# Row sums of squares by products with a column of ones, and another order of loads, in the first stage of a hybrid diffusion backbone

## The chip, the cores and the metric

One core of one Trainium2 chip runs the whole kernel. The metric is the device time of one execution, in microseconds (us). TensorE is called PE here (its weight loads, which overlap its products, PEld), VectorE DVE, ScalarE ACT, GpSimd POOL, and SyncE, which issues most of the transfers, SP.

## What is computed

Two layers over 512 latent tokens x and 256 context tokens ctx, each 1024 wide. Every layer normalizes each token by the root of its mean square, scales and shifts it by vectors that come from a conditioning vector, and feeds a mixer; layer 0 is a retention mixer, layer 1 a gated MLP.

```python
def rmsnorm(x, g):
    y = x * lax.rsqrt(jnp.mean(x * x, axis=-1, keepdims=True) + NORM_EPS)
    return y * g

shift_x, scale_x, gate_x = jnp.split(silu(c) @ ada_w[i] + ada_b[i], 3, axis=-1)
shift_c, scale_c, gate_c = jnp.split(silu(c_ctx) @ ada_w[i] + ada_b[i], 3, axis=-1)
hx = rmsnorm(x, norm_g[i]) * (1 + scale_x) + shift_x
hc = rmsnorm(ctx, norm_g[i]) * (1 + scale_c) + shift_c
...
qx, kx, vx, zx = retention_project(hx, w_in)     # layer 0
qc, kc, vc, zc = retention_project(hc, w_in)
```

The change lies in what leads up to the first products of `retention_project` (the queries and keys of head 0).

## The kernel before, in words

All activations lie transposed: features on the 128 partitions, tokens along the free axis. x is kept as four tiles `xq[t, g]` (t: half of the tokens, 256 each; g: half of the features, four blocks of 128), ctx as two tiles `cq[g]`. Weights and activations are split into a high part (rounded to float32r, a cast on ACT) and a low part (the rest, a subtraction on DVE), and every product of weights is three products: low by high, high by low, high by high (`mm3`).

The first stage does, in the order of its text on each engine (PE, ACT and DVE are pinned to that order there):

- **Row sums.** `flips` transposes a 128-token piece of x with four PE transposes (against `ident`) into a PSUM bank, and `squares` takes the sum of squares along the free axis on ACT, with an accumulator. `inverse` adds the two halves, takes root and reciprocal; `spread` broadcasts the result over the partitions with a product against `ident` and copies it out (`rs[t]`). ctx gets the same in the loop, at kb = 2 and 3 (`half_rows`).
- **Conditioning.** `ada0_mm(kb)` multiplies the silu of both conditioning vectors (`cpad`) by a block of 1 MB of `ada_w`, eight products that use 32 columns of the array each; `ada0_cols(kb)` transposes the copied result with two transposes and makes, on DVE, the scale `gs0` and shift `sh0` for feature block kb.
- **Coming of a block.** `come((kb, th))` multiplies block kb of x by scale and `rs`, adds the shift into the high part on ACT, and makes the low part on DVE.
- **Plain products.** `plain(kb, th, nhs)` multiplies that block by its weights, six passes for each of two weight halves `nh` and each half `th` of tokens. The loop runs over kb = 1 to 7; products of ctx (`th` = 2) follow at kb = 5, 6, 7.
- **Fills.** `fill(n)` multiplies ones by ones n times: it computes nothing that is used. `N_WARM` = 10 stand at the start, 5, 4 and 5 more between the steps.

The weights of the stage are four blocks of 512 KB (B11, B12, B21, B22 of head 0), loaded by `Q.pump_n` and split whole by `Q.upto`. The order of transfers on SP's queue is the order of the calls: first tile of x, `ident`, second tile, `sv`, conditioning block 0, weight block, the other two tiles of x, weight block, conditioning blocks 1 to 3, ctx, and, from inside the loop, the rest. `ada0_load(kb)` puts block kb into a place that later holds something else (`ADA_AT`), so a later load waits for an earlier block's use.

Of the kernel before, what the change touches and what calls it, by code (L numbers as in the profile page):

```python
# [14 lines left out]
P = 128  # L15
D = 1024
# [52 lines left out]
def hybrid_kernel(ctx, tc, xT_d, cT_d, cv_d, sv_d, rows_d, ada0_d, adag_d, w_d, rope_d, dec_d, ws_d, id_d, out_d):  # L69
# [69 lines left out]
    class Stream:  # L139
# [3 lines left out]
        def __init__(self):  # L143
            self.items, self.loads, self.raws, self.left, self.tiles = [], [], {}, {}, {}
            self.free, self.stage, self.done, self.sent, self.at = [], 0, 0, 0, -1
            self.gate = self.limit = self.cap = None

# [10 lines left out]
        def load(self, key, slots, stage, parts):  # L158
            self.loads.append((key, slots, stage, parts))

# [274 lines left out]
    ADA_AT = ("oS1", "oS2", "oS4", "oA22", "oS1", "oS2", "oS4", ("w4", "g1"))  # L435
# [12 lines left out]
    load(xq[0, 0], xT_d[:, 0:4, 0:HS])  # L448
    load(ident, id_d)
    load(xq[0, 1], xT_d[:, 4:8, 0:HS])  # L450
    load(sv, sv_d)
    ada0_load(0)
    Q.stage = 1
    Q.pump_n(1)
    load_x(1)
    Q.pump_n(1)
    for kb in (1, 2, 3):
        ada0_load(kb)
    for g in range(2):
        load(cq[g], cT_d[:, 4 * g:4 * g + 4, :])  # L460
# [49 lines left out]
    def squares(pq, s):  # L510
        act.activation(t2("junk0"), pq, AF.Square, accum_out=s)

    def flips(src, g, i, s):

        pq = pt()
        for k in range(4):
            pe.transpose(pq[:, k * P:k * P + P], src(4 * g + k, i), ident)
        squares(pq, s[:, g, i:i + 1])
        return pq

    def inverse(s):
        dve.tensor_tensor(s[:, 0, :], s[:, 0, :], s[:, 1, :], ALU.add)
        act.activation(s[:, 1, :], s[:, 0, :], AF.Sqrt, bias=eps, scale=1.0 / D)
        dve.reciprocal(s[:, 1, :], s[:, 1, :])

    def spread(s, name):

        pr = pt((P, HS), tag="tm")
        for i in range(2):
            mm(pr[:, i * P:i * P + P], s[:, 1, i:i + 1].to_broadcast([P, P]), ident, start=True, stop=True)  # L530
# [14 lines left out]
    def ada0_cols(kb, e):  # L545
# [6 lines left out]
        dve.tensor_tensor(gs0[:, kb, :], s[:, 0, :], adab0[:, 1, kb, :], ALU.add)  # L552
        dve.tensor_tensor(sh0[:, kb, :], s[:, 1, :], adab0[:, 0, kb, :], ALU.add)
        dve.scalar_tensor_tensor(gs0[:, kb, :], gs0[:, kb, :], 1.0, g0[:, kb, :], ALU.add, ALU.mult)
# [70 lines left out]
    def half_rows(src, g, s):  # L625
        for i in range(2):
            flips(src, g, i, s)

    def by_half(src, name, n=0):
        s = sq[name] = st([P, 2, 2], f"sq{name}", name="sq")  # L630
        for g in range(2):
            half_rows(src, g, s)
            if g == 0:
                fill(n)
# [62 lines left out]
    for low in lows:  # L697
        low()
# [927 lines left out]
```

## Time and profile before

| | |
|---|---|
| median of 3 runs | 875.37 us (874.91 to 875.52) |
| the profiled execution | 875.18 us, its span 873.4 us |
| PE busy | 862.0 us, 99% of the span |
| DVE, ACT busy | 708.6 us, 472.3 us |
| moved | 153.80 MB, mean 176 GB/s |

The profile groups instructions by engine and by the names of their tiles. Busy time of PE is modelled, since products overlap; the start of a weight load is the better mark of when PE got to an instruction. Almost every line reads L55, the helper through which instructions go. In the trace a float32 product is two passes and counts twice; a transpose and a float32r product count once. In slices of 1/40 of the span the transfers are dense only in the first two:

```
DMA  9941761972695596758175722446435045045602
GB/s 332 393 136 62 241 219 59 301 253 97 213 370 145 192 314 220 258 167 303 42 254 188 232 85 77 146 167 217 146 122 176 17 146 191 7 142 194 94 28 97
```

### The profile page before, as it was taken

What the parts mean: (1) busy time and instruction counts of PE and PEld (TensorE: products, weight loads), DVE (VectorE), ACT (ScalarE), POOL (GpSimd) and SP (SyncE); (2) the same over time, 40 slices, a digit from 0 to 9 for tenths busy, and PEclk for the clock granted to TensorE, in tenths of its full rate; (3) what the DMA queues carried; (4) which work ended last, traced back from release to release, by engine and by line L of the source; (5) the groups of instructions that cost most, each with busy time, mean ns of one, the idle gap of its engine ahead of it and who ended that gap; (6) DMA issues with size and microseconds to landing.
All of it is one profiled execution on the core that took longest, in us unless ns stands there. A gap on an engine that the chain in (4) does not pass through costs nothing.

```text
span 873.4 us, 14635 instructions
## 1 busy us (share of the span) xinstructions
PE 862.0 (99%) x5670; PEld 777.3 (89%) x5670; DVE 708.6 (81%) x998; ACT 472.3 (54%) x763; POOL 62.6 (7%) x100
## 2 busy tenths in 40 slices
PE   8999999999999999999999999999999999999996
PEld 6898899898889888999989898888999899899895
DVE  2689979988696987878688869978898578779976
ACT  5466444553524576536362559785865455255345
POOL 0000210110121020000000010102000000000200
PEclk9999999999999999999999999999999999999999
DMA  9941761972695596758175722446435045045602
GB/s 332 393 136 62 241 219 59 301 253 97 213 370 145 192 314 220 258 167 303 42 254 188 232 85 77 146 167 217 146 122 176 17 146 191 7 142 194 94 28 97
DMA packets 77094, 153.80 MB, mean 176 GB/s; under 512 B 8032, under 2 KB 35040, under 8 KB 77024
## 3 DMA queue, kind: packets, MB, share of 16 engines
q1 hardware_dynamic: 68736, 128.53, 44.6%
q0 software_dynamic: 8000, 24.13, 8.4%
q8 instruction: 44, 0.72, 0.3%
q14 instruction: 26, 0.21, 0.1%
q10 hardware_dynamic: 288, 0.20, 0.1%
HBM read 128.71 MB, written 24.12 MB: 175 GB/s over the span
## 4 chain that ended last, share of the span: by engine, by line
PE 93%; ACT 2%; DVE 2%; DMA 2%; issue 0%; SPq 0%; ACTq 0%
PE pst L55 93%; DMA xq<-in_xT_dram 2%; DVE hl L55 1%; ACT hl L55 1%; ACT f L55 1%; ACT oA L55 0%; ACT junk L55 0%; DVE o L55 0%; DVE xq L55 0%; ACT o L55 0%; DVE cq L55 0%; DVE raw L55 0%; ACT oS L55 0%; DVE gs L55 0%; ACT fss L55 0%
## 5 line engine op out<-in xcount | busy, mean ns | idle before, releaser
L55 DVE TENSOR_TENSOR hl<-raw,hl 128x1024 fp32r<-128x1024 f32 x195 | 237.3, 1223 | 71.8 <-ACT hl L55 71.1
L55 ACT CAST hl<-raw 128x1024 fp32r<-128x1024 f32 x195 | 203.6, 1049 | 156.9 <-DVE raw L55 63.1
L55 PE MATMUL pst<-oS,hl 128*128 128x256 f32 x1104 | 134.1, 280 | 0.5 <-ACT oS L55 0.4
L55 PE MATMUL pst<-hl,oS 128*128 128x512 f32 x576 | 134.2, 390 | 0.1
L55 PEld LDWEIGHTS pst<-oS,hl 128*128 128x128 f32 x1104 | 130.9, 188 | 1.3 <-ACT oS L55 0.9
L55 PEld LDWEIGHTS pst<-hl,oS 128*128 128x128 f32 x576 | 107.9, 188 | 23.2 <-DVE oS L55 0.5
L55 PE MATMUL pst<-oA,hl 128*128 128x256 f32 x936 | 117.8, 281 | 0.2
L55 PEld LDWEIGHTS pst<-oA,hl 128*128 128x128 f32 x936 | 112.7, 188 | 2.4 <-issue 0.4
L55 DVE TENSOR_TENSOR raw<-raw 128x1024 f32<-128x1024 f32 x92 | 111.5, 1222 | 0.9
L55 PE MATMUL pst<-hl,oA 128*128 128x512 f32 x408 | 95.8, 390 | 0.0
L55 PE MATMUL pst<-og,hl 128*128 128x256 f32 x768 | 92.8, 280 | 0.0
L55 PEld LDWEIGHTS pst<-og,hl 128*128 128x128 f32 x768 | 90.9, 188 | 0.8 <-issue 0.4
L55 PEld LDWEIGHTS pst<-hl,oA 128*128 128x128 f32 x408 | 76.2, 188 | 15.5
L55 ACT COPY snap<-pst 128x512 f32<-128x512 f32 x84 | 49.1, 585 | 43.0 <-PE pst L55 41.9
L55 PE MATMUL pst<-hl,ya 128*128 128x512 f32 (+1 forms) x300 | 68.5, 381 | 0.0
L55 PEld LDWEIGHTS pst<-hl,ya 128*128 128x128 f32 x300 | 54.6, 188 | 10.7
L55 PE MATMUL pst<-v,ph 128*128 128x512 f32 x192 | 59.4, 391 | 0.0
L55 DVE TENSOR_TENSOR snap<-pst,snap 128x512 f32<-128x512 f32 x63 | 42.8, 688 | 5.7 <-PE pst L55 5.5
L55 ACT CAST ph<-pf 128x512 fp32r<-128x512 f32 x24 | 14.9, 620 | 52.1 <-DVE pf L55 49.7
L55 PEld LDWEIGHTS pst<-v,ph 128*128 128x128 f32 x192 | 36.1, 188 | 7.0
L55 DVE SCALAR_TENSOR_TENSOR acc<-pst,gate,acc 128x256 f32<-128x256 f32 x64 | 29.1, 480 | 13.6 <-PE pst L55 13.4
L55 PE MATMUL pst<-v,pl 128*128 128x512 f32 x96 | 37.9, 395 | 0.0
(196 smaller groups left out, 1011.9 us busy)
## 6 DMA issues: line engine op xcount, KB each, us to landing
raw<-in_w_dram SPq DMA_DIRECT2D x224, 256.0 KB, 4.2
bg<-in_adag_dram SPq DMA_DIRECT2D x32, 512.0 KB, 5.3
ada_w<-in_ada_dram SPq DMA_DIRECT2D x16, 512.0 KB, 8.7
raw<-in_w_dram SPq DMA_DIRECT2D x16, 512.0 KB, 3.7
bg<-in_dec_dram SPq DMA_DIRECT2D x12, 512.0 KB, 5.5
v<-snap POOLq DMA_DIRECT2D x16, 256.0 KB, 4.8
z<-snap POOLq DMA_DIRECT2D x16, 256.0 KB, 5.6
v<-v SPq DMA_DIRECT2D x8, 512.0 KB, 4.7
```

The costliest lines, as they stand in the source:

```text
L55: made = op(*args, **kw)
```

## The change

The squares are taken of x as it lies, on ACT for two of a tile's four blocks and on DVE for the other two; a product with the squares as stationary side and one column of ones as moving side then sums over features into a column of PSUM, for 128 tokens at a time, accumulated over both tiles. No transposes of x or ctx are left. All four tiles of x are loaded first on SP; `ident` and `sv` go to ACT's queue. The first two weight blocks are loaded in slices of columns (one, one, and two of their four 128-column groups) between conditioning blocks, and are split in the same slices. Block 0 and 1 of x are multiplied by `rs` before the scale is known (`ready`), and `first_come` applies scale and shift together on ACT. `ada0_mm` moves in PE's order, the third and fourth weight block are split later, ctx is loaded later and its row sums are taken at kb = 4. There are 61 fills in place of 24.

```diff
+        def begin(self, ks, parts):
+            k0, k1 = ks[0] * P, ks[-1] * P + P
+            for i, (b, kh) in enumerate(parts):
...
+                load(self.raws[key].rearrange("p (s n) -> p s n", s=2)[:, :, k0:k1],
+                     w_d[b:b + 2, :, kh * 512 + k0:kh * 512 + k1].rearrange("s p n -> p s n"))
+
+        def halve(self, i, ks, late=None):
...
+            split((part(hl[:, 0, :]), part(hl[:, 1, :])), part(self.raws[q, at]), late)
...
-    ADA_AT = ("oS1", "oS2", "oS4", "oA22", "oS1", "oS2", "oS4", ("w4", "g1"))
+    ADA_AT = ("oS1", "oS2", "oS4", "oA22", ("w4", "g1"), "oS1", "oS2", "oS4")
...
-    load(xq[0, 0], xT_d[:, 0:4, 0:HS])
-    load(ident, id_d)
-    load(xq[0, 1], xT_d[:, 4:8, 0:HS])
-    load(sv, sv_d)
+    nc.scalar.dma_start(ident, id_d)
+    nc.scalar.dma_start(sv, sv_d)
+    load_x(0)
+    load_x(1)
     ada0_load(0)
-    Q.stage = 1
-    Q.pump_n(1)
-    load_x(1)
-    Q.pump_n(1)
-    for kb in (1, 2, 3):
-        ada0_load(kb)
-    for g in range(2):
-        load(cq[g], cT_d[:, 4 * g:4 * g + 4, :])
+    Q.stage, Q.cap = 1, 2
+    FIRST = ((2, 0), (0, 0))
+    Q.begin((0,), FIRST)
+    ada0_load(1)
+    Q.begin((1,), FIRST)
+    ada0_load(2)
+    Q.begin((2, 3), FIRST)
+    ada0_load(3)
+    ada0_load(4)
...
+    def squares(src, g, sums):
+        for j in range(2):
+            y, x = t2("squares"), src[:, 2 * j:2 * j + 2, :]
+            if j == 0:
+                act.activation(y.rearrange("p (k n) -> p k n", k=2), x, AF.Square)
+            else:
+                dve.tensor_tensor(y.rearrange("p (k n) -> p k n", k=2), x, x, ALU.mult)
+            for k in range(2):
+                for i in range(2):
+                    mm(sums[i][:, 0:1], y[:, k * HS + i * P:k * HS + i * P + P], ones[:, 0:1], start=(g + j + k == 0),
+                       stop=(g + j + k == 3), skip_group_check=True)
...
+    def first_come(kb, th, lows=()):
...
+        act.activation(h, y, AF.Identity, bias=sh0[:, kb, 0:1], scale=gs0[:, kb, 0:1])
+        for low in lows:
+            low()
+        dve.tensor_scalar(f, y, gs0[:, kb, 0:1], None, ALU.mult)
+        dve.scalar_tensor_tensor(l, f, sh0[:, kb, 0:1], f32(h), ALU.add, ALU.subtract)
...
+    fill(12)
+    for th in range(2):
+        sq[th] = [pt() for i in range(2)]
+        for g in range(2):
+            squares(xq[th, g], g, sq[th])
+            fill(8)
+    for th in range(2):
+        sq[th] = inverse(sq[th], f"sq{th}")
+    for th in range(2):
+        rs[th] = spread(sq[th], f"rs{th}")
+    ready(0, 0)
+    ready(0, 1)
     es = ada0_mm(0)
+    lows = []
     ada0_cols(0, es)
+    fill(7)
+    Q.halve(0, (0,))
+    first_come(0, 0)
+    Q.halve(1, (0,), lows)
+    first_come(0, 1, lows)
+    ready(1, 0)
+    ready(1, 1)
+    plain(0, 0)
     es = ada0_mm(1)
+    Q.pump_n(2)
+    ada0_load(5)
+    for g in range(2):
+        load(cq[g], cT_d[:, 4 * g:4 * g + 4, :])
+    for i in (0, 1):
+        Q.halve(i, (1,))
     plain(0, 1, (0,))
     ada0_cols(1, es)
+    first_come(1, 0)
+    first_come(1, 1)
     plain(0, 1, (1,))
...
+    END = {2: 4, 3: 5, 4: 6}
     for kb in range(1, 8):
         if kb == 3:
-            Q.upto(4)
-        plain(kb, 0)
-        if kb + 1 < 8:
+            Q.upto(3)
+        if kb < 3:
+            plain(kb, 0, (0,))
+            es = ada0_mm(kb + 1)
+            plain(kb, 0, (1,))
+        else:
+            plain(kb, 0)
+        if kb < 7:
             ada0_cols(kb + 1, es)
             come((kb + 1, 0), (kb + 1, 1))
-        if kb in (2, 6, 7):
-            Q.upto({2: 3, 6: 5, 7: 6}[kb])
+        if kb == 5:
+            es = ada0_mm(7)
+        if kb == 1:
+            for i in (0, 1):
+                Q.halve(i, (2, 3))
+        if kb in (3, 6, 7):
+            Q.upto({3: 4, 6: 5, 7: 6}[kb])
+        if kb == 4:
+            sq[2] = [pt((P, HS), tag="tm") for i in range(2)]
+            for g in range(2):
+                squares(cq[g], g, sq[2])
+            sq[2] = inverse(sq[2], "sq2")
         plain(kb, 1)
-        if kb + 2 < 8:
-            es = ada0_mm(kb + 2)
+        if kb in END:
+            es = ada0_mm(END[kb])
...
-        if kb in (2, 3):
-            half_rows(rows_c, kb - 2, sq[2])
```

Three places in the engines' orders follow, as they stand. First PE, from its first instruction to the first plain products (`oA` and `oS` are the high and low parts of x for the two halves of tokens, `hl` the split weights, `adae` the copied conditioning product). Before:

```order
L55 MATMUL pst<-ones 128x128 x10
L55 MATMUL pst<-ident,xq 128x128 x8
L55 MATMUL pst<-ones 128x128 x5
L55 MATMUL pst<-ident,xq 128x128 x8
L55 MATMUL pst<-ada_w,cpad 32x256 x8
L55 MATMUL pst<-ones 128x128 x4
L55 MATMUL pst<-ident,sq 128x128 x2
L55 MATMUL pst<-ident,adae 128x128 x2
L55 MATMUL pst<-ident,xq 128x128 x16
L55 MATMUL pst<-oA_250,hl 128x256 x6
```

The same place on PE in the changed kernel, first its start:

```order
L55 MATMUL pst<-ones 128x128 x22
L55 MATMUL pst<-ones,squares 128x1 x8
L55 MATMUL pst<-ones 128x128 x8
L55 MATMUL pst<-ones,squares 128x1 x8
L55 MATMUL pst<-ones 128x128 x8
```

and, after one more such pair of rows, from the last group of squares on:

```order
L55 MATMUL pst<-ones,squares 128x1 x8
L55 MATMUL pst<-ones 128x128 x8
L55 MATMUL pst<-ident,root 128x128 x4
L55 MATMUL pst<-ada_w,cpad 32x256 x8
L55 MATMUL pst<-ident,adae 128x128 x2
L55 MATMUL pst<-ones 128x128 x7
L55 MATMUL pst<-oA_336,hl 128x256 x12
```

Four groups of eight products with squares, each followed by eight fills, stand where transposes stood, and both spreads come ahead of the first conditioning product.

Second, DVE around the coming of block 2 (`ada_s` is the reduced conditioning, `gs` and `sh` scale and shift). Before:

```order
L55 TENSOR_REDUCE ada_s<-pst 128x4
L55 TENSOR_TENSOR gs_151<-ada_s,sv 128x2
L55 TENSOR_TENSOR sh_152<-ada_s,sv 128x2
L55 SCALAR_TENSOR_TENSOR gs_151<-gs_151,sv 128x2
L55 SCALAR_TENSOR_TENSOR xq<-xq,gs_151,rs_240 128x256
L55 SCALAR_TENSOR_TENSOR xq<-xq,gs_151,rs_306 128x256
L55 SCALAR_TENSOR_TENSOR oA_250<-xq,sh_152,oA_250 128x256
L55 SCALAR_TENSOR_TENSOR oS_308<-xq,sh_152,oS_308 128x256
L55 TENSOR_REDUCE ada_s<-pst 128x4
```

The same block on DVE in the changed kernel:

```order
L55 TENSOR_REDUCE ada_s<-pst 128x4
L55 TENSOR_TENSOR gs_155<-ada_s,sv 128x2
L55 SCALAR_TENSOR_TENSOR gs_155<-gs_155,sv 128x2
L55 TENSOR_TENSOR sh_156<-ada_s,sv 128x2
L55 SCALAR_TENSOR_TENSOR xq<-xq,gs_155,rs_296 128x256
L55 SCALAR_TENSOR_TENSOR xq<-xq,gs_155,rs_301 128x256
L55 SCALAR_TENSOR_TENSOR oA_336<-xq,sh_156,oA_336 128x256
L55 SCALAR_TENSOR_TENSOR oS_342<-xq,sh_156,oS_342 128x256
L55 TENSOR_TENSOR hl<-raw,hl 128x2x256 x2
L55 TENSOR_REDUCE ada_s<-pst 128x4
```

Behind the low parts of block 2 now stand the low parts of the last weight slices, which plain(2, ...) needs.

Third, PE around kb = 4 (`oA_585` and `oA_587` hold the second half of features; `root` is the root of a sum). Before:

```order
L55 MATMUL pst<-ada_w,cpad 32x256 x8
L55 MATMUL pst<-ident,sq 128x128 x2
L55 MATMUL pst<-oA_555,hl 128x256 x12
L55 MATMUL pst<-ident,adae 128x128 x2
L55 MATMUL pst<-oA_557,hl 128x256 x12
L55 MATMUL pst<-ada_w,cpad 32x256 x8
```

The same place on PE in the changed kernel:

```order
L55 MATMUL pst<-ada_w,cpad 32x256 x8
L55 MATMUL pst<-oA_585,hl 128x256 x12
L55 MATMUL pst<-ident,adae 128x128 x2
L55 MATMUL pst<-ones,squares 128x1 x16
L55 MATMUL pst<-oA_587,hl 128x256 x12
L55 MATMUL pst<-ada_w,cpad 32x256 x8
L55 MATMUL pst<-ident,root 128x128 x2
```

The products with squares of ctx stand between the transposes of conditioning 5 and plain(4, 1); the transposes of ctx stood at kb = 2 and 3.

More of the change, by code (lines that the diff above doesn't have):

```diff
@@ L159, in load @@
             self.loads.append((key, slots, stage, parts))
+        def begin(self, ks, parts):
+            k0, k1 = ks[0] * P, ks[-1] * P + P
+            for i, (b, kh) in enumerate(parts):
+                key, slots, stage = self.loads[i][:3]
+                if ks[0] == 0:
+                    self.free.remove(slots[i])
+                    self.raws[key] = st([P, 1024], slots[i], name="raw")
+                    self.left[key] = [slots[i], sum(it[0] == key[0] and key[1] in it[2] for it in self.items)]
+                    self.sent += 1
+                load(self.raws[key].rearrange("p (s n) -> p s n", s=2)[:, :, k0:k1],
+                     w_d[b:b + 2, :, kh * 512 + k0:kh * 512 + k1].rearrange("s p n -> p s n"))
+        def halve(self, i, ks, late=None):
+            q, name, uses, at, place = self.items[i]
+            if ks[0] == 0:
+                self.tiles[i] = self.begun[i] = split_tile(q[0])
+                self.done += 1
+            part = lambda x: x.rearrange("p (s n) -> p s n", s=2)[:, :, ks[0] * P:ks[-1] * P + P]
+            hl = self.begun[i]
+            split((part(hl[:, 0, :]), part(hl[:, 1, :])), part(self.raws[q, at]), late)
+            if ks[-1] == 3:
+                self.drop(q, uses)
         def pump_n(self, n):
@@ L508, in hybrid_kernel, with inverse @@
     sh0 = st([P, KT, 2], "sh0")
[L510 to L524, printed above, removed]
+    def squares(src, g, sums):
[9 more added lines that the diff above has]
+                       stop=(g + j + k == 3), skip_group_check=True)
+    def inverse(sums, name):
+        r = st([P, 2], name, name="root")
+        for i in range(2):
+            act.activation(r[:, i:i + 1], sums[i][:, 0:1], AF.Sqrt, bias=eps, scale=1.0 / D)
+        dve.reciprocal(r, r)
+        return r
     def spread(s, name):
@@ L529, in spread @@
         for i in range(2):
-            mm(pr[:, i * P:i * P + P], s[:, 1, i:i + 1].to_broadcast([P, P]), ident, start=True, stop=True)
+            mm(pr[:, i * P:i * P + P], s[:, i:i + 1].to_broadcast([P, P]), ident, start=True, stop=True)
         rs = st([P, HS], name)
@@ L552, in ada0_cols @@
         dve.tensor_tensor(gs0[:, kb, :], s[:, 0, :], adab0[:, 1, kb, :], ALU.add)
+        dve.scalar_tensor_tensor(gs0[:, kb, :], gs0[:, kb, :], 1.0, g0[:, kb, :], ALU.add, ALU.mult)
         dve.tensor_tensor(sh0[:, kb, :], s[:, 1, :], adab0[:, 0, kb, :], ALU.add)
[L554 removed]
     hc = st([P, 2, KT, HS], "hc", F32R)
```

49 lines of the change are left out of this document (12 added, 37 removed).

## The prediction

> **What bounds the kernel now.** First the page: the span, the engines' busy shares, and the chain that ended last.
>
> ```profile
> span 873.4 us, 14635 instructions
> PE 862.0 (99%) x5670; PEld 777.3 (89%) x5670; DVE 708.6 (81%) x998; ACT 472.3 (54%) x763; POOL 62.6 (7%) x100
> PE 93%; ACT 2%; DVE 2%; DMA 2%; issue 0%; SPq 0%; ACTq 0%
> ```
>
> TensorE (PE) carries 93% of the chain. Then that chain in order of time, behind the first stage: two long pieces are PE following PE, without a wait.
>
> ```profile
> 74.87 447.85 PE pst L55 x2840
> ```
> ```profile
> 542.44 318.61 PE pst L55 x2120
> ```
>
> From this I read that what the first stage loses or wins reaches the end one for one: the order of every engine behind it is unchanged, and PE has no idle time there in which a delay could vanish. So the change is judged at one mark, the first product of the stage behind it, at 59.63 us (the timeline of the weight loads):
>
> ```profile
> 59.63 2.58 PEld L55 LDWEIGHTS pst<-hl,oA 128*128 128x128 f32 x12
> ```
>
> PE works in the order of its text. Its time at the mark is therefore the sum of its passes and of its waits, and I take the change as differences in that sum. The waits of weight loads between 5 and 24 us, by who ended them (us in all, times, longest):
>
> ```profile
> PEld pst L55 <- DMA xq<-in_xT_dram: 1.8, 3, 0.8
> PEld pst L55 <- DMA ada_w<-in_ada_dram: 1.4, 2, 1.0
> PEld pst L55 <- ACT oS L55: 0.9, 1, 0.9
> PEld pst L55 <- ACT junk L55: 0.8, 1, 0.8
> PEld pst L55 <- issue: 0.4, 1, 0.4
> PEld pst L55 <- DVE oS L55: 0.3, 1, 0.3
> PEld pst L55 <- DVE hl L55: 0.3, 1, 0.3
> ```
>
> Without "issue" that is 5.5 us, and it is all that a better order of loads can win on PE before 24 us; behind 24 us PE hardly waits in this stage.
>
> **Fills: +8.3 us.** A fill is a product of ones with ones, put there to pass time. A float32 product is two passes in the trace, so ten fills are x20 below, and five are x10:
>
> ```profile
> 1.05 3.93 PEld L55 LDWEIGHTS pst<-ones 128*128 128x128 f32 x20 [1.05 <-DVE eps L55]
> ```
> ```profile
> 6.18 1.20 PEld L55 LDWEIGHTS pst<-ones 128*128 128x128 f32 x10
> ```
>
> The first twenty passes, at the start, are slow (3.93 us). The ten at 6.18 take 1.20 us; less one load's own 0.19 us over nine steps that is 0.112 us a pass. Before there are 10+5+4+5 = 24 fills, now 10+12+4x8+7 = 61. The 37 new ones are 74 passes: 74 x 0.112 = 8.3 us. They are in PE's own order, so they cost nothing only where PE would wait anyway. It would not wait that long: the first tile of x lands 4.3 us after its issue at 0.74, and transfers then stream at 340 GB/s and more (the windows of 5 us; columns: length, busy us of PE, its loads, DVE, ACT, POOL, then clock, DMA share, GB/s).
>
> ```profile
> xq<-in_xT_dram SPq DMA_DIRECT2D x1, 512.0 KB, 4.3
> ```
> ```profile
> 5.00:10.00 5.00, 3.96 (x36) 3.06 (x34) 0.16 (x1) 2.95 (x10) 0.00 (x0) 1.00 1.00 340
> 10.00:15.00 5.00, 3.68 (x31) 2.80 (x32) 2.21 (x7) 2.88 (x8) 0.00 (x0) 1.00 1.07 373
> ```
>
> With the four tiles first, the other three (1.57 MB) and ident and sv (0.12 MB) need 1.69/0.34 = 5.0 us more, so the last tile is there at about 10 us. Before it came at 5.51 + 9.31 = 14.82, in the chain of the stage:
>
> ```profile
> 5.51 9.31 DMA xq<-in_xT_dram
> ```
>
> PE gets to the last tile's products much later, as these rows add up: twenty slow passes to 4.8, 24 passes of fill(12) to 7.5, three tiles of products (3 x 16 passes at 0.08, below, 3.8 us) and three fill(8) (48 passes, 5.3 us): 16.6 us. So the fills stand on PE's path, not under a wait. The last products and fill(8) end at 19.7. Two spreads (0.5 each, the second row below), the conditioning product ada0_mm(0) (1.0), waits for copies (0.7), transposes (0.2) and fill(7) (1.5) put the first weight product at 24.1. The first row is that product before, at 15.7:
>
> ```profile
> 15.69 0.78 PEld L55 LDWEIGHTS pst<-oA,hl 128*128 128x128 f32 x6
> ```
> ```profile
> 17.60 0.52 PEld L55 LDWEIGHTS pst<-ident,sq 128*128 128x128 f32 x4
> ```
>
> **Transposes of x and ctx go: -5.1 us.** Their weight loads, by form:
>
> ```profile
> L55 PEld LDWEIGHTS pst<-ident,xq 128*128 128x128 f32 x32 | 3.4, 141 | 1.9 <-DMA xq<-in_xT_dram 1.8
> ```
> ```profile
> L55 PEld LDWEIGHTS pst<-ident,cq 128*128 128x128 f32 x16 | 1.7, 141 | 0.8 <-DMA ada_w<-in_ada_dram 0.4 <-issue 0.4
> ```
>
> 3.4 + 1.7 = 5.1 us; the rest of the conditioning and all weight products stay in number.
>
> **Products with a column of ones: +7.7 us.** Each of the six tiles (four of x, two of ctx) gets 8 products, so 48, or 96 passes, each a load of 128x128 weights for one moving column. No row shows that form. The nearest above is a fill, with the same kind of weights and 128 columns moved: 0.112 us. The nearest below are loads of 32 columns:
>
> ```profile
> 9.09 0.19 PEld L55 LDWEIGHTS pst<-ada_w,cpad 128*32 128x32 f32 x8 [0.80 <-ACT junk L55]
> ```
>
> Eight of them in 0.19 us, with 0.11 for one (the mean of their group), start (0.19 - 0.11)/7 = 0.012 us apart. I take 0.08, nearer to the fill, whose weights have the same size: 96 x 0.08 = 7.7 us, with ends 1.2 and 10.8.
>
> [...]
>
> **Waits that go: -5.5 us**, the list above. Their place is taken by fills.
>
> **New waits: +9.0 us.** The rows for them, of DVE, then of ACT (columns: busy, mean ns), and one turn of conditioning on DVE:
>
> ```profile
> L55 DVE TENSOR_TENSOR hl<-raw,hl 128x1024 fp32r<-128x1024 f32 x195 | 237.3, 1223 | 71.8 <-ACT hl L55 71.1
> ```
> ```profile
> L55 DVE TENSOR_TENSOR rope_a<-rope_a,rope_b 128x256 f32<-128x256 f32 x32 | 12.2, 422 | 0.3
> ```
> ```profile
> L55 DVE SCALAR_TENSOR_TENSOR xq<-xq,gs,rs 128x256 f32<-128x256 f32 x16 | 7.1, 483 | 1.6 <-ACT rs L55 1.2
> ```
> ```profile
> L55 DVE TENSOR_TENSOR cq<-cq 128x512 f32<-128x512 f32 x4 | 2.8, 689 | 0.0
> ```
> ```profile
> L55 ACT ACTIVATE oA<-xq,sh 128x256 fp32r<-128x256 f32 x12 | 5.7, 504 | 15.3 <-DVE xq L55 15.2
> ...
> L55 ACT ACTIVATE junk<-o 128x512 f32<-128x512 f32 x7 | 4.4, 631 | 6.3 <-DVE o L55 6.3
> ...
> L55 ACT COPY adae<-pst 128x256 f32<-128x256 f32 x8 | 2.9, 363 | 3.1 <-PE pst L55 3.1
> ```
> ```profile
> 26.01 0.17 DVE L55 TENSOR_REDUCE ada_s<-pst 128x4 f32<-128x16 f32 x1 [1.98 <-PE pst L55]
> ...
> 26.61 0.88 DVE L55 SCALAR_TENSOR_TENSOR xq<-xq,gs,rs 128x256 f32<-128x256 f32 x2
> ```
>
> A turn: transposes end on PE, 0.2 us later the reduction, 0.6 us to gs and sh, 0.8 for x of both halves of tokens, 0.2 until ACT's high part, 0.8 for the two low parts, 2.6 us on DVE. A half plain product is 0.7 us on PE, a whole one 1.4, a conditioning product 1.0:
>
> ```profile
> 27.30 0.59 PEld L55 LDWEIGHTS pst<-ada_w,cpad 128*32 128x32 f32 x16
> 28.30 1.47 PEld L55 LDWEIGHTS pst<-oA,hl 128*128 128x128 f32 x12 [0.41 <-ACT oS L55]
> ```
>
> - Ahead of kb = 1: behind ada0_mm(1) stand its copy (0.2 to the bank's end, 0.4), the cast of a weight slice (0.4), two low parts (0.4 each), 0.6 to gs and sh, 0.5 for the high part: 2.9 us. PE has 0.7 + 0.2 + 0.7 = 1.6. Wait 1.3, and 0.4 more for the low part: 1.7.
> - Ahead of kb = 2: DVE does a turn (2.6), then the low part of the 128x2x256 slice behind its cast (0.2 + 0.7): 3.5 us, while PE has plain(1,1), 1.4. Wait 2.1. Queued behind on PE: ada0_mm(3).
> - In kb = 4: the low part of the fourth weight block now stands behind come(4). From the end of turn 4's transposes, DVE has the third block's low part (1.1), the turn's own 2.4, 0.6 until the cast is done, and 1.2: 5.3 us. PE has plain(3,1) 1.4, ada0_mm(5) 1.0, 0.7 of waits that it had before too, and half a product, 0.7: wait 1.5.
> - The squares of ctx in kb = 4 stand behind come(5): ACT squares after 0.2 + 0.6 + 0.5 + 0.9 + 0.5 = 2.7 us. PE's next instructions are the products of those squares, and plain(4,1), ready long before, is queued behind them. Wait 2.7. Before, the transposes of ctx had data that lay there.
> - Smaller ones up to the first weight product: 1.0 (0.1 for rs, 0.6 for the copy, 0.3 for the low part).
>
> 1.7 + 2.1 + 1.5 + 2.7 + 1.0 = 9.0. The range of this is 3 (the slices and B22 converted earlier than I lay them) to 11.
>
> Costed at nothing: the extra DMA pieces (the slices of weights): what is needed until kb = 2 (x, three conditioning blocks, the slices, 6.4 MB) takes 6.4/0.36 = 18 us from 3 us on, and PE gets to the last of it 7 us behind the first weight product, at 31; without that cover a piece costs its 0.13 MB/0.36 = 0.4 us; the squares of x on ACT and DVE, under the fills; conditioning moved in PE's order, same count.
>
> **Sum.** 8.3 - 5.1 + 7.7 - 5.5 + 9.0 = +14.4 us. The profiled execution took 875.18 us (span 873.4 and 1.8 around it), the median of the runs is 875.37, so the bases agree. 875.2 + 14.4 = 889.6, taken as 889.5.
>
> **Rivals.**
> - *Short passes are cheap.* At 0.012 us the products cost 1.2 in place of 7.7: 883. For it: the row of 32 columns. Against: the weights here are four times as wide. Chance 0.16.
> - *They cost as much as a fill or more*: 10.8 in place of 7.7, 892.5. For it: transposes take 3.4/32 = 0.106 and fills 0.112. Chance 0.17.
> - *New waits mostly hidden*, 3 in place of 9: 883.5. For it: DVE is busy only 0.16 to 2.2 of 5 us early on; against: the waits are chains behind PE's own transposes. Chance 0.07.
> - *PE falls back to its starting speed* in kb = 4, where a wait of 2.7 is followed by short passes. The row of the start gives 3.93 us for 20 passes that take 2.2 later, a loss of 1.7; once or twice, say 2.5: 892. Before, PE's loads were busy only 3.06 and 2.80 of 5 us between 5 and 15 us, and passes stayed at 0.11. Chance 0.10. [...]
> - *Faster: the stage follows the transfers.* Place: the last tile of x. If PE stood ready when it lands (10 us, not 14.82), the whole stage would move 4.6 to 4.8 us forward, less 0.9 for ctx products above transposes (2.6 - 1.7): 871.5. It decides at 0.05 us a pass: the 72 warm fill passes and 48 product passes ahead of the last products must be done between 4.8 and 10.7 us. The fill row says 0.112. Chance 0.04.
> - *The order of loads does not bring x early* (small pieces on the queue): x landing as late as 14.8 changes nothing, as PE is at its last products at 16.6; it is inside the forecast. A balance of all terms near zero, 875: chance 0.02.
>
> **How the numbers follow.** The forecast, 889.5 (alone 886 to 892), has 0.44. The range takes in cheap and dear products, hidden waits and the slow clock: from 881.5 (883 less 1.5 for waits) to 895 (892.5 and 2.5). A measurement of this kernel tells some 0.2% (1.75 us) from no change. Faster 0.04, within 0.02, slower 0.94.
>
> **What would show it.** PE's 24 + 64 + 14 warm fill passes at 0.11 each, without a wait before the products; the first 128x256 product near 24; PE waiting for DVE and ACT at kb = 1, 2 and 4, about 2 us each; loads of squares spaced 0.05 to 0.11; the mark near 74. I am wrong if PE waits for x ahead of the products, or if the mark comes before 62.

## The result, and the profile after

The changed kernel takes 899.96 us (median of 4 runs, 898.59 to 902.58) against 875.41 us: a ratio of 1.0285, with an interval of 1.0257 to 1.0313. The direction is the predicted one. The size is not: the forecast was 889.5 us and its range ended at 895. The profiled execution took 898.61 us.

First the page of the changed kernel: its span, busy shares and the chain that ended last.

```profile
span 896.8 us, 14886 instructions
...
PE 880.8 (98%) x5792; PEld 796.0 (89%) x5792; DVE 713.7 (80%) x1009; ACT 470.4 (52%) x752; POOL 62.7 (7%) x100
...
PE 94%; DVE 2%; ACT 2%; DMA 0%; issue 0%; ACTq 0%; DVEq 0%
```

The span grew by 23.4 us, PE still carries the chain, and the loads now have 0% of it where they had 2%. Next the timeline of PE's weight loads (start, length, instructions, and in brackets the wait ahead of them).

```profile
1.05 7.05 PEld L55 LDWEIGHTS pst<-ones 128*128 128x128 f32 x44 [1.05 <-DVE eps L55]
8.02 1.87 PEld L55 LDWEIGHTS pst<-ones,squares 128*128 128x128 f32 x16
9.81 1.87 PEld L55 LDWEIGHTS pst<-ones 128*128 128x128 f32 x16
...
20.52 1.87 PEld L55 LDWEIGHTS pst<-ones 128*128 128x128 f32 x16
...
26.85 0.19 PEld L55 LDWEIGHTS pst<-oA,hl 128*128 128x128 f32 x1
...
32.80 0.19 PEld L55 LDWEIGHTS pst<-oA,hl 128*128 128x128 f32 x1 [1.19 <-ACT oA L55]
...
39.65 0.77 PEld L55 LDWEIGHTS pst<-oA,hl 128*128 128x128 f32 x6 [2.15 <-DVE hl L55]
...
51.98 0.77 PEld L55 LDWEIGHTS pst<-oA,hl 128*128 128x128 f32 x6 [1.43 <-DVE hl L55]
...
55.82 6.21 PEld L55 LDWEIGHTS pst<-ones,squares 128*128 128x128 f32 x32 [2.87 <-ACT squares L55]
61.91 2.68 PEld L55 LDWEIGHTS pst<-oA,hl 128*128 128x128 f32 x12
...
83.30 1.68 PEld L55 LDWEIGHTS pst<-hl,oA 128*128 128x128 f32 x8
```

The mark, the first product with 128x512, stands at 83.30 us in place of 59.63: 23.67 us later, the whole loss of the profiled executions (898.61 less 875.18 is 23.4). So it arose ahead of the mark, and nothing was made up or lost behind it. Three things are to be read here. A group of 16 passes with the column of ones takes 1.87 us, exactly as long as 16 passes of fills: (1.87 - 0.19)/15 = 0.112 us a pass. The four waits at kb = 1, 2 and 4 are there (1.19 and 0.33; 2.15; 1.43; 2.87), near the sizes predicted. And at 55.82 the 32 passes for ctx take 6.21 us, where 32 at the start's 0.112 make 3.6, and the twelve loads of plain(4, 1) behind them 2.68 in place of 1.47 us.

The waits of weight loads between 5 and 30 us, in the form that the prediction used: no transfer is among them any more.

```profile
PEld pst L55 <- ACT adae L55: 1.0, 1, 1.0
PEld pst L55 <- issue: 0.4, 1, 0.4
PEld pst L55 <- DVE oA L55: 0.4, 1, 0.4
PEld pst L55 <- ACT rs L55: 0.2, 1, 0.2
```

Why these passes took longer shows in windows of 3.43 us around kb = 4, a third of the time for which the clock was low (length, busy us of PE, its loads, DVE, ACT, POOL, then the granted clock, DMA share, GB/s).

```profile
49.74:53.17 3.43, 2.07 (x14) 1.61 (x13) 1.74 (x3) 1.20 (x2) 0.00 (x0) 1.00 0.88 272
53.17:56.60 3.43, 0.80 (x8) 0.78 (x8) 3.13 (x10) 1.95 (x4) 0.00 (x0) 1.00 0.47 156
56.60:60.03 3.43, 3.43 (x18) 3.43 (x18) 0.37 (x1) 0.00 (x0) 0.00 (x0) 0.50 0.00 0
60.03:63.46 3.43, 3.43 (x17) 3.43 (x18) 0.17 (x1) 0.52 (x2) 0.00 (x0) 0.50 0.00 0
63.46:66.89 3.43, 3.43 (x24) 1.94 (x24) 0.00 (x0) 0.02 (x1) 0.00 (x0) 0.51 0.03 5
66.89:70.32 3.43, 3.43 (x36) 2.68 (x37) 2.42 (x7) 2.04 (x5) 0.00 (x0) 1.00 0.01 2
```

PE's granted clock is 0.50 for 10.2 us, though PE is busy all that time. It falls behind a window in which PE was busy 0.80 of 3.43 us. In the kernel before it is 1.00 in every window of 5 us up to 80.

### The profile page after: what moved, and what is told of

Its sections match the earlier page's. It is cut to its first block, busy times and chain, and to the rows that moved or that the text cites. A ratio compares the mean times of both kernels' runs of the same rounds, so it can differ in the third digit from the quotient of the medians.

```text
span 896.8 us, 14886 instructions
## 1 busy us (share of the span) xinstructions
PE 880.8 (98%) x5792; PEld 796.0 (89%) x5792; DVE 713.7 (80%) x1009; ACT 470.4 (52%) x752; POOL 62.7 (7%) x100
## 4 chain that ended last, share of the span: by engine, by line
PE 94%; DVE 2%; ACT 2%; DMA 0%; issue 0%; ACTq 0%; DVEq 0%
PE pst L55 94%; DVE hl L55 1%; ACT hl L55 1%; ACT oA L55 1%; ACT f L55 0%; DMA ada_w<-in_ada_dram 0%; DVE o L55 0%; ACT junk L55 0%; DVE xq L55 0%; DVE gs L55 0%; ACT o L55 0%; DVE cq L55 0%; DVE raw L55 0%; DVE oA L55 0%; ACT fss L55 0%
## 5 line engine op out<-in xcount | busy, mean ns | idle before, releaser
L55 DVE TENSOR_TENSOR hl<-raw,hl 128x1024 fp32r<-128x1024 f32 (+2 forms) x199 | 237.6, 1200 | 72.4 <-ACT hl L55 71.8
L55 ACT CAST hl<-raw 128x1024 fp32r<-128x1024 f32 (+2 forms) x199 | 204.3, 1031 | 159.2 <-DVE raw L55 62.9
L55 PE MATMUL pst<-oA,hl 128*128 128x256 f32 x936 | 120.3, 284 | 4.6 <-DVE hl L55 3.2
```

The costliest lines, as they stand in the source:

```text
L55: made = op(*args, **kw)
```

## The experiments

Every run stands against the kernel before on the same chip, at 875.1 to 875.2 us; the second number given is the ratio to it, with its interval. That a product with one moving column costs as much as a fill is read from the rows above. For the clock, the first theory was that the wait of 2.87 us and the passes behind it bring it down together; the rivals were that passes with one moving column count as idle by themselves, or that the other waits of the new order do it.

**Squares of ctx made ahead**, so that their products need not wait. `made` makes them, `summed_up` multiplies.

```diff
+        if kb == 4:
+            ysc = [made(cq[g]) for g in range(2)]
         if kb < 7:
             ada0_cols(kb + 1, es)
...
-                squares(cq[g], g, sq[2])
+                summed_up(ysc[g], g, sq[2])
```

> The mark is the first 128x512 product of the next stage: 59.6 us before, 83.3 in the changed kernel. Here the squares of ctx are made on ACT and DVE ahead of come(5), so that PE need not wait for them; PE's order is as in the changed kernel. Theory: the wait of 2.9 us and the short passes behind it together brought the clock to 0.5 for 10 us; without the wait the 32 passes take 3.6 us at the full clock. That saves 2.9 + 2.6 + 2.1 (the products behind), 7.6 us: 892.4, mark near 75.7, clock 1.00. Rival: short passes alone count as idle; then the clock falls anyway and only some 2.9 us are saved: 897.

Measured: 899.77 us (895.51 to 899.83), 1.0270 (1.0247 to 1.0293). Neither theory nor rival gives that time. The wait was gone, but in the profiled execution the clock fell twice. Windows of that run, around two of the waits that were left:

```profile
37.55:40.98 3.43, 1.48 (x12) 1.28 (x12) 3.22 (x8) 1.93 (x4) 0.00 (x0) 1.00 0.89 345
40.98:44.41 3.43, 3.43 (x25) 1.93 (x24) 0.00 (x0) 0.38 (x1) 0.00 (x0) 0.52 1.05 370
...
51.27:54.70 3.43, 2.06 (x17) 1.26 (x10) 2.80 (x5) 3.02 (x6) 0.00 (x0) 1.00 0.84 261
54.70:58.13 3.43, 3.38 (x18) 3.29 (x17) 2.61 (x10) 0.91 (x2) 0.00 (x0) 0.51 0.62 198
```

The first fall, at 41.1 us, came behind the wait of 2.15 us at kb = 2 and lasted 3.4 us. The second came at 54.8, behind the wait of 1.42 us for the fourth weight block and 0.8 us ahead of the first pass of ctx; it lasted 13.7 us, the passes of ctx taking 7.16 us. So this run does not tell whether such passes bring the clock down by themselves. It shows falls behind waits of 2.15 and 1.42 us, and a clock that stayed at 0.50 while the passes ran. One of the four executions took 895.51.

**Twelve fills ahead of the products of ctx**, in the place of the wait.

```diff
+            for i in range(12):
+                mm(sq[2][0][:, P:HS], ones, ones, start=True, stop=True, skip_group_check=True)
             for g in range(2):
                 squares(cq[g], g, sq[2])
```

> The changed kernel with 12 more fills (24 passes, 2.7 us) on PE ahead of the products with squares of ctx, where it waited 2.9 us. Theory (the idle stretch brought the clock down): the clock stays, the short passes take 3.6 in place of 6.2 and what follows 2.1 less: 4.7 us saved, 895, mark 78.6. Rival (short passes alone count as idle): the clock falls during or behind them, the time stays at 899 to 901.

Measured: 895.29 us (894.69 to 895.64), 1.0229 (1.0212 to 1.0246). A row of its timeline, then its windows of 3.43 us.

```profile
55.68 3.65 PEld L55 LDWEIGHTS pst<-ones,squares 128*128 128x128 f32 x32
```
```profile
52.84:56.27 3.43, 3.43 (x32) 3.28 (x30) 2.94 (x10) 1.95 (x4) 0.00 (x0) 1.00 0.53 161
56.27:59.70 3.43, 3.43 (x32) 3.43 (x32) 0.56 (x1) 0.47 (x2) 0.00 (x0) 1.00 0.02 5
59.70:63.13 3.43, 3.43 (x27) 2.41 (x25) 0.17 (x1) 0.02 (x1) 0.00 (x0) 0.51 0.00 0
```

With the clock up, the 32 passes take 3.65 us. But the window that they fill but for its last 0.4 us, 3.43 of 3.43 us busy and no wait in it, is followed by one at 0.51. So in this run the clock fell behind passes with one moving column without a wait of PE, as the rival has it. That the median is the theory's 895 is luck: the clock fell, and the mark stood at 79.97, not at 78.6.

**No fills among the products of x.**

```diff
-    fill(12)
+    fill(0)
...
-            fill(8)
+            fill(0)
```

> The changed kernel without fill(12) and without the four fill(8): 88 passes less, 9.9 us at 0.112. Theory (fills stand on PE's path): PE then waits for tiles of x, the last products end near 12.9 us, the spread starts near 13.2 in place of 22.3: 9 us saved, 891, mark 74.3 (with the slow clock at kb = 4 still in). [...]

Measured: 897.82 us (896.11 to 897.89), 1.0255 (1.0240 to 1.0270). Its timeline and one of its windows:

```profile
6.60 12.10 PEld L55 LDWEIGHTS pst<-ones,squares 128*128 128x128 f32 x64 [1.36 <-ACT squares L55]
```
```profile
11.83:15.26 3.43, 3.43 (x18) 3.43 (x18) 0.17 (x1) 0.26 (x1) 0.00 (x0) 0.50 1.06 378
```

From 8.4 us on, behind the first sixteen of them, the 64 passes run at 0.50; they take 12.10 us in place of 7.1. Leaving out 88 fill passes won 2.1 us where they cost 9.9, and the theory's 891 was missed: with the fills, in the changed kernel, the clock read 1.00 over the products of x and they took 0.112 us a pass.

**Row sums of ctx undone**, by transposes at kb = 2 and 3 as before.

```diff
+        if kb in (2, 3):
...
+            half_rows_c(kb - 2, sqc)
...
-        if kb == 4:
-            sq[2] = [pt((P, HS), tag="tm") for i in range(2)]
-            for g in range(2):
-                squares(cq[g], g, sq[2])
```

> The changed kernel with the row sums of ctx as before (transposes at kb = 2 and 3, accumulated squares on ACT). Theory: the part of ctx costs 2.9 (wait) + 6.2 (passes) + 2.1 (slow clock behind them) - 1.7 (the transposes that come back) = 9.5 us: 890.5, mark 73.8, clock 1.00 throughout. Rival (the slow clock comes from elsewhere, such as the waits at kb = 1, 2 and 4): it stays, and at most 5 us are saved: 895.

Measured: 889.55 us (888.45 to 891.25), 1.0167 (1.0151 to 1.0183). In its profiled execution the clock was 1.00 throughout and the mark stood at 72.91. That is near the theory's 890.5. The products of ctx, their wait and the slow clock, less the transposes that come back, make 10.4 of the 24.6 us.

**Sides swapped**: a block of ones is the stationary side and 256 columns of squares move, so the sum lands on every partition and no spread is left.

```diff
+    ones_r = st([P, P], "ones_r", F32R)
+    act.copy(ones_r, ones)
...
-                for i in range(2):
-                    mm(sums[i][:, 0:1], y[:, k * HS + i * P:k * HS + i * P + P], ones[:, 0:1], start=(g + j + k == 0),
-                       stop=(g + j + k == 3), skip_group_check=True)
+                mm(bank[:, 0:HS], ones_r, y[:, k * HS:k * HS + HS], start=(g + j + k == 0), stop=(g + j + k == 3),
+                   skip_group_check=True)
```

> The changed kernel with the sides of the row sums swapped: a 128x128 block of ones (float32r) is the stationary side and 256 columns of squares (float32r) move, so the sum lands on every partition and no spread is left. Order, fills and the wait for the squares of ctx stay. Theory (the loss of 24 us is mostly the form of the products: 96 passes, each a load for one moving column, and the clock that falls while they run): the products of x are 16 passes of about 0.12 = 1.9 us in place of 7.1, those of ctx 8 in place of 32 passes, 0.9 in place of 6.2, three spreads (1.5) go, and with long moving sides the clock stays at 1.00 in kb = 4, which gives back some 2.5 more: 899.9 - 5.2 - 5.3 - 1.5 - 2.5 = 885.5 us. Rival (it is the wait of 2.9 us ahead of the products of ctx that brings the clock down, whatever follows it): the clock falls to 0.5 behind the wait all the same, and some 5 us of this stay: 890.5.

Measured: 887.38 us (887.28 to 887.50), 1.0142 (1.0128 to 1.0156), between the two, nearer to the theory. A row of its timeline and its windows in kb = 4:

```profile
8.46 0.54 PEld L55 LDWEIGHTS pst<-squares,ones_r 128*128 128x128 f32 x4
```
```profile
47.27:50.70 3.43, 0.69 (x5) 0.36 (x3) 3.01 (x10) 1.95 (x4) 0.00 (x0) 1.00 0.99 315
50.70:54.13 3.43, 3.43 (x16) 3.43 (x17) 1.79 (x2) 0.47 (x1) 0.00 (x0) 0.50 0.40 128
54.13:57.56 3.43, 3.43 (x38) 2.47 (x40) 2.77 (x7) 1.58 (x4) 0.00 (x0) 1.00 0.00 0
```

A pass now costs (0.54 - 0.19)/3 = 0.117 us, but there are 16 for x in place of 64. Behind the wait (2.87 us here too) the clock still falls, to 0.50 at 50.7 us, so the rival holds for the fall; the theory holds for its length: with products of 256 columns behind the wait the clock is back after one window, with one-column passes (the changed kernel) it took three.

**Swapped, without the 12 and four times 8 fills.**

> As the run with swapped sides, but the 12 fills ahead of the products of x and the four times eight among them are left out. Theory (these 88 passes stand on PE's path; with products that keep the clock up they are not needed): PE follows the transfers of x, the last of which lands at 10.2 us, its products end near 11.5 in place of 16.5, and the clock holds: 5 us less than with the fills, about 880.5. Rival (in the pauses of 1 to 1.5 us between the tiles of x the clock falls to 0.5, as it did in the run without fills and with one moving column): what follows up to 20 us runs at half speed, 4 to 5 us are lost again, the time is that of the swapped run with fills, about 885.

Measured: 883.65 us (882.35 to 884.99), 1.0100 (1.0086 to 1.0113), between the two. The first weight product came at 16.19 in place of 21.05 us, 4.9 us earlier, where the theory had 5. Then the clock fell behind the wait of 2.15 us at kb = 2 too, for 3.4 us, and 1.5 of it were given back: the mark moved from 71.60 only to 68.27. The slow passes of the rival were there as well, among the tiles of x:

```profile
6.83 1.78 PEld L55 LDWEIGHTS pst<-squares,ones_r 128*128 128x128 f32 x8 [1.43 <-ACT squares L55]
```

That is (1.78 - 0.19)/7 = 0.23 us a pass, twice the 0.117 above, while the granted clock of that stretch reads 1.00.

**The kernel before with swapped row sums alone**, and then with the squares made a step ahead of their products:

> The kernel before with nothing changed but its row sums: the transposes of x and ctx give way to squares of the tiles as they lie and products with a 128x128 block of ones as stationary side, 256 columns of squares moving, no spreads; order of loads, fills, conditioning and weights stay. Theory (the idea of the change pays if the form of the products is right and nothing else is moved): 48 passes of transposes (5.1 us) and three spreads (1.5) go, 24 passes of 0.12 (2.8) come, of which the part of x is half hidden under the waits for loads of x: 1.5 to 3.5 us less than before, about 873. Rival (the stage ahead of the first weight product follows the loads, so that only the part of ctx counts: 1.7 and 0.5 go, 0.9 come): 874.1, no difference that can be told.

> The kernel before with its row sums by a block of ones against 256 columns of squares, as in the run with that alone, but with the squares made a step ahead of their products: those of the second half of x behind block 0's coming and their products behind plain(0, 0), those of ctx ahead of plain(2, 1) and plain(3, 1). Theory (that run lost its time to a wait of 3.58 us that brought the clock down, and to waits of 1.6 to 2.7 us for squares of ctx, and not to the form): both go, no clock is lost, and of the transposes and spreads that are gone (6.6 us against 2.8 for the products) the part that does not lie under waits for loads is won, 1.3 for ctx at least: 873 us. Rival (the reciprocal of 128x256 on DVE, 1.75 us in place of 0.17, takes the place of the spread in the chain of the second half of tokens): nothing is won, 875.

Measured: 880.53 us (879.80 to 881.57), 1.0067 (1.0053 to 1.0081), and 880.47 us (879.48 to 881.72), 1.0062 (1.0049 to 1.0075). All four expectations missed. A row of each timeline, of the first and of the second:

```profile
15.72 0.50 PEld L55 LDWEIGHTS pst<-squares,ones_r 128*128 128x128 f32 x2 [3.58 <-ACT squares L55]
```
```profile
16.47 0.98 PEld L55 LDWEIGHTS pst<-oA,hl 128*128 128x128 f32 x6 [3.72 <-ACT squares L55]
```

PE stands for 3.6 or 3.7 us at about 15 us, and behind it the clock is at 0.50, for 6.8 us in the first run and 3.4 in the second. In the kernel before, two groups of transposes of x, 0.86 us each, stood in that stretch, and no wait over 0.83 us. At kb = 2 PE waits 1.66 us for squares of ctx still in the second run, since ACT and DVE get to them late, and the clock falls once more, for 3.4 us. The form alone is no gain in the old order.

**The reordered version**: loads and slices as in the changed kernel, swapped sums, few fills, and the old places of conditioning and of the splits of the third and fourth block.

```diff
-    fill(12)
+    fill(6)
...
-            fill(8)
+            fill(4 if (th, g) != (1, 1) else 3)
...
+        plain(kb, 0)
+        if kb + 1 < 8:
             ada0_cols(kb + 1, es)
...
+        if kb in (2, 6, 7):
+            Q.upto({2: 3, 6: 5, 7: 6}[kb])
...
         plain(kb, 1)
+        if kb + 2 < 8:
+            es = ada0_mm(kb + 2)
```

> Loads of x first and weights in slices as in the changed kernel, row sums with swapped sides, 6, 4, 4, 4 and 3 fills in place of 12, 8, 8, 8 and 8 and then 6 in place of 7, conditioning products two blocks ahead and the splits of the third and fourth weight block at the places of the kernel before, the squares of ctx made ahead of kb = 5's block and multiplied behind plain(4,1). Theory (with cheap products, few fills and the old places of conditioning and splits, the order of loads is worth what it saves in waits): against the swapped run, 5 us for fills and 5 for the waits at kb = 1, 2 and 4 go: 875, with an error of 3. Rival (the first weight product waits for x, conditioning and weights together, and PE loses in waits there what it does not spend in fills): 880.

Measured: 874.88 us (874.51 to 875.68), 0.9998 (0.9989 to 1.0006): the theory's number, and no difference from the kernel before. The clock was never low.

**Two runs of 16 passes for ctx in place of one of 32.**

```diff
+            summed_up(ysc[0], 0, sq[2])
+        plain(kb, 1)
+        if kb == 4:
+            summed_up(ysc[1], 1, sq[2])
```

> The changed kernel with the squares of ctx made ahead of the coming of block 5, so that PE need not wait for them, and their products in two runs of 16 passes: the first tile's ahead of plain(4, 1), the second's behind it. Theory (a run of products with one moving column counts as a pause for PE's clock; 32 passes are too long a pause, 16 between long products are not, as the four runs of 16 between fills at the start kept the clock at 1.00): the clock holds, the wait of 2.9 us goes, the passes take 2 x 1.9 in place of 6.2 us, and what runs at half clock behind them, about 2.5 us, goes: 899.9 - 2.9 - 2.4 - 2.5 = 892 us. Rival (something else in kb = 4 brings the clock down, the other waits there for instance): it falls again, and only the wait and a part of the rest goes, 897 to 899, as in the run with the squares made ahead and one run of 32.

Measured: 898.84 us (894.28 to 900.88), 1.0264 (1.0238 to 1.0289): the rival's number, and its reason. In the profiled execution the clock had fallen before the first of these passes, twice:

```profile
37.05:40.48 3.43, 1.48 (x12) 1.28 (x12) 3.19 (x9) 1.94 (x4) 0.00 (x0) 1.00 0.94 365
40.48:43.91 3.43, 3.43 (x25) 1.93 (x24) 0.23 (x1) 0.38 (x1) 0.00 (x0) 0.52 1.05 361
...
50.77:54.20 3.43, 2.06 (x23) 1.11 (x12) 2.80 (x6) 3.16 (x6) 0.00 (x0) 1.00 0.82 248
54.20:57.63 3.43, 3.38 (x17) 3.30 (x17) 2.41 (x8) 0.50 (x2) 0.00 (x0) 0.51 0.68 211
```

The falls, at 40.6 and 54.2 us, came behind the waits of 2.15 us at kb = 2 and of 1.43 us for the fourth block, with PE busy 1.48 and 2.06 of the 3.43 us ahead of them. After the first fall, with plain and conditioning products behind it, the clock was back in 3.4 us; after the second, with one-column passes among the products behind it, it took 17.1.

**The old places of conditioning and splits alone**, all else as in the changed kernel; then the same with the squares of ctx made ahead.

> The changed kernel with its fills, its row sums with one column (those of ctx at kb = 4 behind their wait) and its loads, but conditioning products two blocks ahead and the splits of the second weight slices and of the third and fourth block earlier, at the places of the kernel before. Theory (the new waits are what the moved conditioning and the late splits cost, and nothing else stands behind them): the waits of 1.19 + 0.33 at kb = 1, 2.15 at kb = 2 and 1.43 for the fourth block go, 5.1 us; the clock still falls at the products of ctx: 894.8 us. Rival (PE waits for DVE and ACT wherever the work stands, since they must do it in those 25 us): half comes back as other waits, 897.5 us.

> The run with the old order of conditioning and splits, with the squares of ctx also made ahead, ahead of the coming of block 5: no wait over 1 us is left around kb = 4, and 32 passes with one moving column (3.6 us at full clock) run there in one piece. In the runs so far the clock was low for 3.43 us or a multiple of it, so it seems to be set slice by slice of 3.43 us. Theory (a slice falls that holds little but pauses and passes with one column; 3.6 us of them fill a slice of 3.43 only where the slices happen to lie so): in most executions the clock holds, as each slice has some long products: 893.9 - 2.9 for the wait - 0.9 for the passes - 1.9 for what ran at half clock = 888 us, with single executions some 4 us above. Rival (one-column passes bring the clock down whatever lies around them): it falls every time, and only the wait goes: 891.

Measured: 893.87 us (892.63 to 895.55), 1.0220 (1.0205 to 1.0236), and 888.16 us (887.02 to 888.30), 1.0146 (1.0132 to 1.0160). The first is near its theory: the three waits were gone, a smaller one in kb = 4 grew from 0.48 to 0.93, and the clock was low for 6.8 in place of 10.2 us. The second meets the theory's time, but not its reason: the clock did not hold in the profiled execution. Windows of that run:

```profile
50.17:53.60 3.43, 3.43 (x32) 3.43 (x31) 1.05 (x3) 0.94 (x4) 0.00 (x0) 1.00 0.58 192
53.60:57.03 3.43, 3.43 (x25) 1.93 (x24) 0.00 (x0) 0.40 (x2) 0.00 (x0) 0.50 0.03 7
```

No wait for data lies in the first of them, only 2 us of one-column passes and 1.4 of plain(4, 1), and the clock fell, for one window. That answers the question that the split run left open: here the clock fell behind these passes without a wait for data. The mean clock of the four executions was 0.996 three times, the profiled one among them, and 0.999 once, which fits a fall in three of the four; only one has a trace.

**A version that beats both**, in two steps from the reordered one. The reciprocals of the second half of tokens are cut in two around the coming of block 0, the squares of ctx are made at kb = 3, one fill less, and, in the first step only, the third weight block is split at kb = 1.

```diff
+    dve.reciprocal(rs[0], rs[0])
     ready(0, 0)
+    dve.reciprocal(rs[1][:, 0:P], rs[1][:, 0:P])
...
     first_come(0, 0)
+    dve.reciprocal(rs[1][:, P:HS], rs[1][:, P:HS])
+    ready(0, 1)
```

> The reordered run with three edits: the reciprocals of the second half of tokens are cut in two and taken around the coming of the first block, the squares of ctx are made at kb = 3, and the third weight block is split at kb = 1 in place of kb = 2; one fill less. Theory (the waits left in the reordered run are 1.0 us ahead of the first weight product, which two reciprocals of 1.75 us on DVE hold up, 1.0 for squares of ctx and about 0.9 at kb = 4): they go, 2.5 to 3 us: 872. Rival (the first weight product is held by the load of conditioning block 0, which lands near 14 us, and the rest turns into other waits): 874.9, as the reordered run.

> As the tuned run, but the third weight block is split at kb = 2 again, since its load landed at 29.28 us there and ACT, waiting for it, held up the copy of conditioning (PE's wait of 2.90 us at 30.64). Theory (that wait was the price of this edit alone, and the other two edits had won 1.3 us up to the first weight products and 1.0 at the squares of ctx): against the reordered run, 874.9, 2.3 us less: 872.6. Rival (the transfers, which run at 400 GB/s until 40 us, hold the stage wherever PE gets ahead of them): the gain turns into waits for loads, 874.5.

Measured: 875.61 us (874.75 to 877.60), 1.0010 (1.0001 to 1.0019), a miss, and 873.52 us (873.19 to 874.30), 0.9982 (0.9973 to 0.9991). The first step's loss is one row of its timeline on ACT, and the row of PE that follows from it:

```profile
29.28 1.04 ACT L55 CAST hl<-raw 128x1024 fp32r<-128x1024 f32 x1 [3.06 <-DMA raw<-in_w_dram]
```
```profile
30.64 0.20 PEld L55 LDWEIGHTS pst<-ident,adae 128*128 128x128 f32 x2 [2.90 <-ACT adae L55]
```

Split a block earlier, the third weight block is not there yet: ACT waits for its load, and the copy of conditioning behind the cast comes late. With that edit taken back the mark stands here:

```profile
57.83 2.58 PEld L55 LDWEIGHTS pst<-hl,oA 128*128 128x128 f32 x12
```

That is 1.8 us ahead of the kernel before, and the median is 1.67 us below it. So the order of loads and squares of x as they lie are worth about 0.2% together with these edits, once form, fills and waits are mended; without them (the reordered version) no difference could be told.

## Why the prediction was wrong, and where it was right

The sum of the prediction against the trace, in us; each measured term is from the rows above.

| step | predicted | measured |
|---|---|---|
| fills | +8.3 | +8.3 (0.112 a pass, no wait ahead of them) |
| transposes | -5.1 | -5.1 |
| products with a column of ones | +7.7 | +13.2 (x: 64 x 0.112 = 7.1; ctx: 55.82 to 61.91, 6.1) |
| waits that go | -5.5 | -5.5 |
| new waits | +9.0 | +9.6 (1.5; 2.15; 1.4; 2.9; smaller ones 1.6) |
| slow clock behind the products of ctx | not in the sum | +2.1 (plain(4, 1) 1.2, the conditioning product behind it 0.9) |
| together | +14.4 | +22.6, of 23.7 at the mark (1.1 not assigned) |

- **What bounds** was right: the shift at the mark is the loss, to 0.3 us. (That transfers are dense only in the first two slices of the span is not so: the twelfth has 370 GB/s. No term of the sum rests on it.)
- **Fills** were right, with their reason: PE never waited for x. What I did not see is that they were not idle time only. In the run without them the clock was 0.50 over the products of x from 8.4 us on, with them 1.00, so the 9.9 us of the 88 passes could not be had back by taking them out (2.1 us).
- **The products** are the step that failed, in two ways. "I take 0.08, nearer to the fill" was too low: the row that I called nearest gave the price itself, 0.112, and the 32-column row had no say in it. That is 3.1 us over the 96 passes (10.8 in place of 7.7). The dear-passes rival priced it right but had 0.17. The second way is the clock, next.
- **The slow clock** was named as a rival ("a wait of 2.7 is followed by short passes"), with 0.10 and a price of 2.5 us. It came: 2.5 us on the products of ctx (6.1 in place of 3.6) and 2.1 behind them, 4.6 in all. I argued against it that PE's loads had been busy only 2.80 of 5 us before without a fall; but those passes moved 128 or 256 columns each, and I counted one-column passes as work like any other. In two runs the clock fell to 0.50 behind them with PE busy 3.43 of 3.43 us (twelve fills ahead; no wait over 1 us), and in the run without fills it stayed at 0.50 as long as they ran, from 8.4 to 18.6 us. In the changed kernel itself the fall came behind the wait, and lasted 10.2 us with the passes behind it, where it lasted 3.4 in the swapped run. Had I priced both, the sum would have been 875.2 + 14.4 + 3.1 + 4.6 = 897.3, above the range and 1.3 from the profiled execution; the forecast's mistake is in the main this one step and its clock, 7.7 of the 10.5 us between forecast and median.
- A pass with one moving column took 0.112 us at full clock (16 in 1.87 us) and 0.22 at 0.50 (32 in 7.16, squares of ctx made ahead).
- A fall came behind a wait of 2.15 us among plain products (the split run, at 40.6 us), and behind passes with one column without a wait for data (the old order with the squares made ahead, at 53.6). Behind the wait of 2.15 us in the changed kernel there was none.
- Worked out from the granted clock in pieces of 0.1 us, the low clock lasts 3.41, 6.83, 10.24, 13.65 and 17.07 us in the profiles of the eleven kernels here whose clock fell, one to five times 3.41. Where it fell twice in an execution, the stretch between is a multiple too: 10.24 us in the run with the squares of ctx made ahead and in the split run, 13.65 in the swapped run without fills, 17.07 in the second of the two runs of the kernel before, 30.72 in the run without fills, that is three, four, five and nine times 3.41.
- **Waits that go** and **new waits** were right in size, each of the four large ones to 0.2 us. The run with the old order took three of them away and won 6.1 us (899.96 to 893.87): 1.5 + 2.15 + 1.4 less 0.45 for one that grew, 4.6, and a shorter fall of the clock. The smaller ones around the first weight product were 1.6, not 1.0 (the list above without "issue"): PE waits 0.97 for the copy of conditioning, a time in which fills stood before.
- **The first weight product** came at 26.85, not 24.1: 2.0 for the 64 passes, and most of the rest for that copy (0.97, where the waits for copies were laid at 0.7 in all).
- **The rival of a faster stage** asked for 0.05 us a pass; with 0.112 it was out, as the fill row said. The version that beats both reaches its first weight product at 15.91 us, no earlier than the kernel before; it wins behind it.

What stays open: whether PE's work in the 3.4 us ahead decides on a fall, and how much it must be. A window with 1.48 us of PE busy fell (the split run, 37.05 to 40.48), and one with 1.56 did not (the run with the old order, 47.23 to 50.65). But the split run also fell behind one with 2.06, of which 0.67 were conditioning products on 32 columns, and two windows with much the same work, part of it conditioning, differ: 1.60 fell (swapped, without fills, 27.19 to 30.60), 1.64 did not (the run without fills, 35.73 to 39.15). That conditioning products count for less is not shown; it was not tried alone. The spread of single runs of the changed kernel (898.59 to 902.58) could come from falls that differ between executions; that is argued, not shown.

## What to carry to other kernels

Sum over partitions with the ones as stationary side and the data moving: here a product with one moving column took 0.112 us a pass, as long as a fill with 128, and needed four times the passes (64 in place of 16 for x), and in two runs the clock fell to 0.50 behind such passes without a wait for data. Before a wait or a run of short products is put among long ones, look in a trace at the granted clock behind it, since a fall added its price to the wait here: 4.6 us behind a wait of 2.87 in the changed kernel, 1.5 behind one of 2.15 in the swapped run without fills. And fills are to be taken out only together with what they carried here: a clock of 1.00 (0.50 from 8.4 us on without them), and the time in which a copy or a load arrives.

## What the runs showed of the hardware that was not expected

- The granted clock was 0.50 with PE busy 3.43 of 3.43 us, in passes with one moving column; such a pass then took 0.22 us (32 in 7.16, squares of ctx made ahead) in place of 0.112.
- The falls lasted 3.41 us or a whole multiple of it, up to 17.07, and the same stretch of instructions fell in one run and not in another (at kb = 2 at 40.6 us in the split run, not there in the changed kernel, whose PE has the same order up to that place).
- A reciprocal on DVE took longer with more elements of a partition: 1.75 us for 128x256, 0.16 for 128x2 (groups of the reordered version), 0.94 for 128x128 (the first of the two steps of the last version), where a subtraction of 128x1024 took 1.2.

```profile
L55 DVE RECIPROCAL dec<-dec 128x256 f32<-128x256 f32 x1 | 1.8, 1752 | 1.1 <-ACT dec L55 1.1
...
L55 DVE RECIPROCAL ss<-ss 128x2 f32<-128x2 f32 x8 | 1.3, 162 | 3.6 <-ACT ss L55 3.6
```

- The first passes of every kernel are slow (twenty took 3.93 us in the kernel before and 4.34 in the swapped run without fills, about 0.2 each), and in the swapped run without fills the passes of x, up to 11.6 us, are so too (0.23 each), while the granted clock of these stretches reads 1.00; the row of the clock does not show the start. How long the start lasts differs between runs: the same 44 passes took 6.37 us in the run with the row sums of ctx undone and 7.80 with the squares of ctx made ahead.
